# Layer 0's FFN by seven block products, with the context chunk computed ahead of them

## The chip, the cores and the metric

The kernel runs on one core of one Trainium2 chip. The time is device microseconds of one execution, from the runs of the kernel; lower is better. The profile is of one further execution.

## What is computed

Two layers of a trunk over 1024 latent tokens and 256 context tokens, width 1024. Each layer has a mixer (attention) and a SwiGLU FFN of hidden width 2816; after layer 1 only the latent tokens are wanted, so only layer 0's FFN handles the context. Cut to what matters here:

```
def swiglu(h, w_in, w_out):
    g, u = jnp.split(h @ w_in, 2, axis=-1)
    return (jax.nn.silu(g) * u) @ w_out

    x = x + g1 * rms_norm(y, norm_g[l, 1])
    h = rms_norm(x, norm_g[l, 2]) * (1.0 + sc2) + sh2
    x = x + g2 * rms_norm(swiglu(h, ffn_w_in[l], ffn_w_out[l]), norm_g[l, 3])
    if need_ctx:                       # layer 0 only
        xc = xc + cg1 * rms_norm(yc, norm_g[l, 1])
        hc = rms_norm(xc, norm_g[l, 2]) * (1.0 + csc2) + csh2
        xc = xc + cg2 * rms_norm(swiglu(hc, ffn_w_in[l], ffn_w_out[l]), norm_g[l, 3])
```

All inputs are float32. The kernel reaches the accuracy by splitting each matmul operand into a high part in fp32r and the rest, and computing high x high, high x low and low x high: three matmuls for each block (`mm3`).

## The kernel before

The tokens lie in three chunks along the free dimension: `a` and `b` (512 latent tokens each) and `c` (the 256 context tokens). Activations are feature-major: 128 features on the partitions, tokens along the columns. Weights come from HBM as tiles of 128 x 1024 (512 KB), are split by a cast on ScalarE (ACT) into the high part and a subtraction on VectorE (DVE) into the low part (`wsplit`), and are the stationary operands.

There are four pools of buffers: `T` (44 tiles of 128 x 1024), `U` (13 of 128 x 512), `S` (small columns) and `b` (the 8 PSUM banks). The profile calls every tile by its pool: `T`, `U`, `S`, `b`; `scr` is scratch in DRAM. All DMAs are issued from SyncE (SP).

The program is recorded first (`Recorder`) and then issued in an order that a planner finds: it runs a list scheduler with its own costs for the instructions, takes on each engine the earliest recorded of those that are ready, and gives out the buffers of a pool in the order in which they were first used in the recording. The order found is fixed for each engine. Work that runs beside the matmuls (residuals, norms) is written as generators; `tick(us)` advances them at points of the recording and so sets where in the recorded order their work stands. `until(f)` only repeats ticks while recording.

**FFN of layer 0** (`OutFFN.run`). After the output projection of the mixer (`p1`: chunks c and a, `p2`: chunk b), `after` makes the residual and the norm of each chunk, high and low parts in `h2`. Then the 22 hidden tiles `j` run: for each chunk `gu` (gate and up, 48 matmuls over 8 features tiles, Silu, product, split) and `down` of the tile before (24 matmuls, whose results DVE adds to `yacc` from PSUM). One load and one split of the three weight tiles serves all three chunks. The last two tiles run chunk by chunk, c first, so that `finish` (residual, then the norm of layer 1) of c and a runs beside the last matmuls.

**FFN of layer 1** (`WinoFFN.run`), chunks a and b only, by the seven block products of the Winograd form of Strassen's scheme. `after` makes seven sets of four operand tiles, each split into high and low: blocks `B11`, `B21` from chunk a, and `B22`, `T1` to `T4` from a and b; these 28 `T` tiles stay to the end of the tiles. For the first `EARLY` (8) tiles the two products that need only chunk a (`early`) are made while b's sets are not there yet, and parked in `EA` in DRAM. `raw` loads the tiles of gate and up, `prep` makes weight sums on GpSimd (POOL) and splits them, `tile` runs the products of one hidden tile (84 matmuls of 512 columns; 60 for a tile whose first two were made early) and stores the activations to `ACT` in DRAM. Then `down_all` runs the seven products of the down projection, `P1, P5, P6, P3, P7, P2, P4`, 11 steps (`HALF`) of 12 matmuls each: `dload` brings halves of activations (256 KB) and weights four steps ahead, `dprep` makes differences of activations on DVE and weight sums on POOL and splits both, two steps ahead. P5 needs the difference of the two halves of an activation tile, P6, P7 and P4 one more each. `finish` of b starts after P7, that of a after P4.

**Between them**, `odd_mixer` of layer 1: the hook in `f0.run` makes its first loads; then `Proj` runs the projections `(i, chunk)` in a fixed order that starts with weights 9 to 12 (`lead`), chunks c and a, then b.

Of the kernel before, what the change touches and what calls it, by code (L numbers as in the profile page):

```python
# [12 lines left out]
F32 = mybir.dt.float32  # L13
F32R = mybir.dt.float32r
I32 = mybir.dt.int32
AF = mybir.ActivationFunctionType
# [3 lines left out]
P = 128  # L20
D = 1024
KT = D // P
# [3 lines left out]
HID = 2816  # L26
NJ = HID // P
# [16 lines left out]
CHUNKS = {"a": (0, 512), "b": (512, 512), "c": (1024, 256)}  # L44
# [1289 lines left out]
def odd_mixer(pr, h, OT, pre_out):  # L1334


    nc, d = pr.nc, pr.d
# [41 lines left out]
    def evac(i, c, ps):  # L1379
# [17 lines left out]
    ws = [d["od_qk"][i] for i in range(13)]  # L1397
    qorder = lambda i: "ab" if i in (0, 1, 2, 3, 5, 6, 7, 8) else "cab"
    lead = (9, 10, 11, 12)
    order = [(i, c) for i in lead for c in "ca"] + [(i, "b") for i in lead] + \  # L1400
        [(i, c) for i in (4, 0, 1, 2, 3, 5, 6, 7, 8) for c in qorder(i)]
    pj = pr.proj(ws, order, h, evac)
    pj.near = N1
# [139 lines left out]
class OutFFN:  # L1543
# [78 lines left out]
    def begin(self):  # L1622
        for k in "gu":
            self.fetch(k, 0)
        for k in "gu":
            self.cv(k, 0)
        for k in "ogu":
            self.fetch(k, k != "o")
# [85 lines left out]
class WinoFFN(OutFFN):  # L1714
# [4 lines left out]

    EARLY = 8
    HALF = NJ // 2

    def __init__(self, *args):
        super().__init__(*args)
        self.hf, self.sets, self.ready = {}, {}, set()
        self.ACT = self.pr.dram([HID, 1024], F32)
        self.EA = self.pr.dram([self.EARLY * P, 1024], F32)


    def put_set(self, name, k, x):
# [7 lines left out]
            self.ready.add(name)  # L1740

    def after(self, c):
        pr, l, nc = self.pr, self.l, self.pr.nc
        n = CHUNKS[c][1]
        y = self.y.pop(c)
        acc2 = pr.accs()
        yield from pr.g_residual(y, self.acc.pop(c), self.xsrc(c), pr.vec(pr.der[l], 1, c), acc2)
        dst = self.view(self.X1, c)
        for i, t in enumerate(y.tiles):
            pr.load(dst[2 * i * P:2 * i * P + 2 * P, :].rearrange("(k p) n -> p k n", p=P),  # L1750
                    t.rearrange("p (k n) -> p k n", n=n))
        cols = pr.rstd(acc2, n, D)
        yield -RSW
        rb = pr.bcast(cols)
        A, Bv = pr.vec(pr.der[l], 2, c), pr.mvec(l, 3, c)

        def norm(kt):
            pr.stt(y[kt], y[kt], A(kt), rb[:, :n])
            nc.scalar.activation(y[kt], y[kt], AF.Identity, bias=Bv(kt))

        self.hf[c] = y
        if c == "a":
            for kt in range(KT):
                norm(kt)
                self.put_set("B11" if kt < 4 else "B21", kt % 4, y[kt])
                if kt % 2:
                    yield 3.0
            return
        a = self.hf["a"]
        for k in range(4):  # L1770
            norm(k)
            norm(k + 4)
            self.put_set("B22", k, y[k + 4])
            pr.sub(a[k], y[k], a[k])
            yield 2.6
            self.put_set("T1", k, a[k])
            pr.tt(y[k], y[k + 4], y[k], ALU.subtract, eng=nc.gpsimd)
            pr.sub(a[k], y[k + 4], a[k])
            self.put_set("T2", k, a[k])
            yield 2.4  # L1780
            pr.tt(a[k + 4], a[k + 4], a[k], ALU.subtract, eng=nc.gpsimd)
            self.put_set("T3", k, y[k])
            self.put_set("T4", k, a[k + 4])
            yield 2.4
        self.hf.clear()
# [12 lines left out]
        pr.tick(2.7)  # L1798

    def begin(self):  # L1800
        for j in range(2):
            self.fetch("g", j)
        self.gsplit(0)

    def gsplit(self, j):
        hi, lo = self.pr.wsplit(self.raws.pop(("g", j)))
# [52 lines left out]
    def tile(self, j):  # L1859
# [40 lines left out]
        def last():  # L1900
            self.prod(x, "T4", u, 0, False)
            if late:
                pr.add(s5, s1, x)
                pr.mul(act[:, 0:512], sa, s5)
            else:
                pr.mul(act[:, 0:512], sa, x)
            pr.later(lambda: pr.load(self.ACT[j * P:(j + 1) * P, :], act))
            self.last = lambda: None
        self.last = last
# [7 lines left out]
    def dload(self, k):  # L1917
# [16 lines left out]
            pr.load(raw, pr.d["ffn_out"][self.l, j * P:(j + 1) * P, r * 512:(r + 1) * 512])  # L1934
            self.wr.setdefault(k, []).append(raw)

        for a in {"P1": [(0, 0)], "P5": [(0, 1)], "P6": [(1, 1)], "P2": [(1, 0)]}.get(p, []):
            act(*a)
        for b in {"P1": [(0, 0)], "P5": [(1, 0), (1, 1)], "P6": [(0, 0)], "P3": [(0, 1)], "P7": [(0, 0), (1, 0)],
                  "P2": [(0, 1)], "P4": [(1, 1)]}[p]:  # L1940
            w(*b)

    def dprep(self, k):
# [14 lines left out]
            x = k1[:, lo]  # L1958
        elif p == "P5":
            x = k1[:, lo]  # L1960
            pr.sub(x, k1[:, hi], x)
            pr.tt(s, raw[0], raw[1], ALU.add, eng=gp)
        elif p == "P6":
            x = k1[:, lo]
# [19 lines left out]
            self.at.pop(t)  # L1984
            self.at.pop(t + H)

    def down_all(self):
        pr, nc, H = self.pr, self.pr.nc, self.HALF
        self.at, self.wr, self.sw, self.dop = {}, {}, {}, {}
        ya, yb = FMs(pr), FMs(pr)  # L1990
# [7 lines left out]
        for k in range(7 * H):  # L1998
# [8 lines left out]
            for f in range(4):  # L2007
# [2 lines left out]
                pr.mm(ps, wh, xs[:, 0:512], new, False)  # L2010
                pr.mm(ps, wh, xs[:, 512:1024], False, False)
                pr.mm(ps, wl, xs[:, 0:512], False, t == H - 1)
            pr.tick(2.7)
            if t < H - 1:
                continue
            if p == "P7":
# [22 lines left out]
                    pr.sq_add(self.acc["a"], ya[f + 4], 512, 2 * f + 1)  # L2039
            if p == "P7":  # L2040
                pr.long(self.finish("b"))
        pr.long(self.finish("a"))

    def run(self, hook=None):
# [1 line left out]
        pr.drain_slow()  # L2046
        self.p1.run((len(first) * KT - 2, self.p2.start))
        self.p2.run((KT - 3, self.begin))
        pr.until(lambda: "B11" in self.ready)
        for j in range(self.EARLY):  # L2050
            self.early(j)
        self.raw(0)
# [6 lines left out]
        while pr.bg:  # L2059
            pr.tick(0)  # L2060
        self.sets.clear()
        self.down_all()


class FMs:
# [16 lines left out]
def program(ctx, nc, tc, d, out):  # L2082
# [22 lines left out]
        t0, n = CHUNKS[c]  # L2105
        pr.store_fm(out[:, t0:t0 + n], x)

    f0 = OutFFN(pr, 0, "cab", OT0, lambda c: src0[c], put2, norm1)
    f1 = WinoFFN(pr, 1, "ab", OT1, lambda c: X2[:, CHUNKS[c][0]:CHUNKS[c][0] + CHUNKS[c][1]], put3, None)
    m0 = even_mixer(pr, h0, OT0, f0.g_pre)  # L2110
    m1 = odd_mixer(pr, h1, OT1, f1.g_pre)
# [107 lines left out]
```

## Time and profile before

| | us |
|---|---|
| median of 3 runs | 3303.39 (3302.07 to 3306.06) |
| the profiled execution | 3301.75 |
| its span (first to last instruction) | 3300.0 |
| PE busy | 3147.5 (95%) |
| DVE busy | 2156.7 (65%) |
| ACT busy | 1525.0 (46%) |
| POOL busy | 841.1 (25%) |

PE is TensorE's matmuls, PEld its weight loads, which overlap them. Times in the rows are microseconds from the start of the span. Every operation of this kernel goes through one recording helper, so all have one source line (L260), and groups are told apart by their tiles. A few per cent of the matmul records are missing, so counts of matmuls in a window are a little low.

### The profile page before, as it was taken

How to read it: one execution, taken by the hardware profiler on the slowest of the kernel's cores; microseconds unless marked ns; L12 is line 12 of the kernel's file. 1: busy time of each engine (PE TensorE's matmuls, PEld its weight loads, DVE VectorE, ACT ScalarE, POOL GpSimd, SP SyncE). 2: the span in 40 equal slices, each digit the busy share in tenths (PEclk: the TensorE clock that was granted, in tenths of full speed). 3: DMA queues.
4: the chain of work that ended last, by engine and by line, in shares of the span. 5: the costliest groups of instructions: out<-in, count | busy, mean ns of one | idle time of the engine just before them, and what ended most of it. 6: DMA issues, size and time to landing. Idle time of an engine off the chain costs nothing.

```text
span 3300.0 us, 45509 instructions
## 1 busy us (share of the span) xinstructions
PE 3147.5 (95%) x16520; PEld 2605.2 (79%) x16520; DVE 2156.7 (65%) x4083; ACT 1525.0 (46%) x3426; POOL 841.1 (25%) x1091
## 2 busy tenths in 40 slices
PE   7999999999999999999998999899999879999997
PEld 5877777887888888888887887667777768888876
DVE  5569888865544444444469765988995675345984
ACT  4359877864411111111124324777896543334352
POOL 2311100015200000000035643773001554322622
PEclk8999999999999999999999999999999989999998
DMA  6263754354111111111114343533134343224732
GB/s 243 68 220 107 218 167 131 109 186 159 64 39 39 39 39 39 39 39 39 39 59 158 106 140 106 144 109 111 53 115 141 141 153 128 77 83 160 254 109 93
DMA packets 153376, 368.29 MB, mean 112 GB/s; under 512 B 14080, under 2 KB 35264, under 8 KB 153152
## 3 DMA queue, kind: packets, MB, share of 16 engines
q1 hardware_dynamic: 153152, 365.39, 33.6%
q8 instruction: 130, 2.13, 0.3%
q14 instruction: 94, 0.77, 0.1%
HBM read 277.97 MB, written 87.36 MB: 111 GB/s over the span
## 4 chain that ended last, share of the span: by engine, by line
PE 75%; DVE 11%; ACT 4%; POOL 3%; issue 3%; DMA 3%; SPq 0%; POOLq 0%; ACTq 0%; DVEq 0%
PE b L260 75%; DVE T L260 6%; DVE U L260 3%; DVE S L260 3%; ACT T L260 2%; ACT U L260 2%; POOL U L260 2%; POOL S L260 1%; DMA T<-in_ada_w_dram 1%; DMA scr<-T 1%; DMA U<-scr 0%; DMA U<-in_ffn_out_dram 0%; DMA T<-scr 0%; POOL T L260 0%; DMA T<-in_ctxT_dram 0%
## 5 line engine op out<-in xcount | busy, mean ns | idle before, releaser
L260 PE MATMUL b<-T,T 128*128 128x512 f32 (+5 forms) x10618 | 2321.4, 370 | 55.2 <-DVE T L260 22.1
L260 PEld LDWEIGHTS b<-T,T 128*128 128x128 f32 (+2 forms) x10618 | 1837.5, 190 | 404.8 <-ACT T L260 41.3
L260 PE MATMUL b<-U,T 128*128 128x512 f32 (+2 forms) x2752 | 692.3, 376 | 7.3 <-DVE U L260 3.2
L260 DVE TENSOR_TENSOR T<-T,T 128x1024 fp32r<-128x1024 f32 (+4 forms) x475 | 499.7, 1078 | 218.8 <-PE b L260 111.3
L260 PEld LDWEIGHTS b<-U,T 128*128 128x128 f32 x2752 | 465.2, 191 | 78.9 <-issue 5.0
L260 POOL TENSOR_TENSOR U<-U,U 128x512 f32<-128x512 f32 (+1 forms) x141 | 195.5, 1389 | 1114.4 <-PE b L260 806.0
L260 ACT CAST T<-T 128x1024 fp32r<-128x1024 f32 (+3 forms) x362 | 300.7, 845 | 359.4 <-PE b L260 245.4
L260 DVE TENSOR_REDUCE S<-b 128x1 f32<-128x512 f32 (+1 forms) x672 | 374.0, 568 | 63.4 <-PE b L260 58.5
L260 DVE TENSOR_TENSOR U<-U,b 128x512 f32<-128x512 f32 (+3 forms) x228 | 143.5, 630 | 415.9 <-PE b L260 405.9
L260 ACT ACTIVATE T<-b,S 128x512 f32<-128x512 f32 (+1 forms) x640 | 385.5, 609 | 47.9 <-DVE S L260 42.8
L260 DVE TENSOR_TENSOR U<-b,U 128x512 fp32r<-128x512 f32 (+3 forms) x528 | 335.4, 646 | 21.0 <-ACT U L260 16.8
L260 PE MATMUL b<-ident,T 128*128 128x128 f32 x1968 | 316.3, 276 | 23.8 <-ACT T L260 13.2
L260 ACT CAST U<-b 128x512 fp32r<-128x512 f32 (+3 forms) x528 | 291.1, 565 | 87.7 <-PE b L260 84.2
L260 PEld LDWEIGHTS b<-ident,T 128*128 128x128 f32 x1968 | 237.8, 141 | 89.1 <-ACT T L260 31.7
L260 DVE TENSOR_TENSOR T<-T,b 128x512 f32<-128x512 f32 (+1 forms) x524 | 283.1, 594 | 17.1 <-PE b L260 17.1
L260 ACT ACTIVATE U<-b 128x512 f32<-128x512 f32 (+1 forms) x104 | 55.0, 531 | 393.5 <-PE b L260 391.5
L260 POOL TENSOR_TENSOR T<-T,T 128x512 f32<-128x512 f32 x146 | 203.3, 1403 | 118.5 <-DVE T L260 104.9
L260 ACT COPY U<-b 128x512 f32<-128x512 f32 (+3 forms) x175 | 96.2, 550 | 171.9 <-PE b L260 170.2
L260 POOL TENSOR_TENSOR T<-U,T 128x512 fp32r<-128x512 f32 (+2 forms) x51 | 66.4, 1302 | 404.6 <-ACT T L260 371.2
L260 ACT CAST T<-U 128x512 fp32r<-128x512 f32 (+3 forms) x166 | 96.4, 585 | 151.7 <-DVE U L260 110.3
L260 ACT ACTIVATE U<-T 128x512 f32<-128x512 f32 (+1 forms) x174 | 96.1, 577 | 90.7 <-DVE T L260 84.5
L260 ACT ACTIVATION_READ_ACCUMULATOR T<-b,S 128x1 f32 x640 | 132.8, 207 | 0.0
(81 smaller groups left out, 1663.8 us busy)
## 6 DMA issues: line engine op xcount, KB each, us to landing
scr<-T SPq DMA_DIRECT2D x144, 512.0 KB
T<-in_ada_w_dram SPq DMA_DIRECT2D x96, 512.0 KB
T<-in_ffn_in_dram SPq DMA_DIRECT2D x96, 512.0 KB
T<-scr SPq DMA_DIRECT2D x90, 512.0 KB
T<-scr SPq DMA_DIRECT2D x132, 256.0 KB
U<-in_ffn_out_dram SPq DMA_DIRECT2D x99, 256.0 KB
T<-in_w_out_dram SPq DMA_DIRECT2D x32, 512.0 KB
T<-in_ffn_out_dram SPq DMA_DIRECT2D x22, 512.0 KB
```

The lines of the kernel that those rows point to most:

```text
L260: f(*args, **kw)
```

## The change

1. Layer 0's FFN becomes a `WinoFFN` too, for a and b. Its context chunk is computed ahead of the products by a new method `context`: for each of the 22 hidden tiles gate, up and the down of the tile before, at 256 columns, the down results accumulated in four PSUM banks over all tiles and then parked in DRAM (`YC`). The weights of gate, up and down are so loaded and split once for the context and again for the products. In layer 0 no tile is early; `context` takes that place. `finish_c` loads the parked sums back after P2.
2. In both layers the difference that P5 needs is made in `tile` for the first 11 tiles and stored to DRAM (`T1`); P5 loads it in place of the second half of the activations, which is now loaded at P7.
3. Layer 1 makes 12 early tiles instead of 8.
4. `down_all` takes the hook and calls it at the start of P4; the ticks of P2 and P4 are 1.8 instead of 2.7; layer 1's first projections run chunks c and b, then a.

```diff
-    order = [(i, c) for i in lead for c in "ca"] + [(i, "b") for i in lead] + \
+    order = [(i, c) for i in lead for c in "cb"] + [(i, "a") for i in lead] + \
...
-    EARLY = 8
     HALF = NJ // 2
...
         self.ACT = self.pr.dram([HID, 1024], F32)
-        self.EA = self.pr.dram([self.EARLY * P, 1024], F32)
+        self.T1 = self.pr.dram([HID // 2, 512], F32)
+        if "c" in self.chunks:
+            self.EARLY = 0
+            self.YC = self.pr.dram([2 * P, 1024], F32)
+        else:
+            self.EARLY = 12
+            self.EA = self.pr.dram([self.EARLY * P, 1024], F32)
...
+    def context(self):
+        pr, nc = self.pr, self.pr.nc
+        n = CHUNKS["c"][1]
+        act, out = {}, None
+        pr.until(lambda: "c" in self.h2)
+        hi, lo = self.h2["c"]
+        for j in range(NJ + 1):
+            if j < NJ:
+                self.cv("o", j)
+                ps = pr.b()
+                for i, kind in enumerate("gu"):
+                    wh, wl = self.conv.pop((kind, j))
+                    pr.mm3(ps[:, i * n:i * n + n], [(wh[:, k * P:(k + 1) * P], wl[:, k * P:(k + 1) * P], hi[k], lo[k])
+                                                    for k in range(KT)])
+                    pr.tick(n / 100)
+                    if j + 1 < NJ:
+                        if not i:
+                            self.fetch("o", j + 1)
+                        self.cv(kind, j + 1)
+                        self.fetch(kind, j + 2)
+                sg, a = pr.U()[:, :n], pr.U(F32R)
+                nc.scalar.activation(sg, ps[:, 0:n], AF.Silu)
+                pr.mul(sg, sg, ps[:, n:2 * n])
+                act[j] = (a[:, 0:n], a[:, n:2 * n])
+                pr.split(sg, *act[j])
+            if j == 0:
+                continue
+            if out is None:
+                out = [pr.b() for _ in range(4)]
+            ah, al = act.pop(j - 1)
+            wh, wl = self.conv.pop(("o", j - 1))
+            for f in range(KT):
+                ps = out[f // 2][:, (f % 2) * n:(f % 2) * n + n]
+                s = slice(f * P, (f + 1) * P)
+                pr.mm(ps, wh[:, s], ah, j == 1 and f % 2 == 0, False)
+                pr.mm(ps, wh[:, s], al, False, False)
+                pr.mm(ps, wl[:, s], ah, False, j == NJ)
+            pr.tick(n / 100)
+        self.h2.pop("c")
+        for i in range(2):
+            y = pr.T()
+            for k in range(2):
+                nc.scalar.copy(y[:, k * 512:(k + 1) * 512], out[2 * i + k])
+            pr.load(self.YC[i * P:(i + 1) * P, :], y)
+
+    def finish_c(self):
+        pr = self.pr
+        n = CHUNKS["c"][1]
+        y = self.yacc["c"] = FM(pr, n, F32)
+        for i, t in enumerate(y.tiles):
+            pr.load(t, self.YC[i * P:(i + 1) * P, :])
+        yield -3.0
+        acc = self.acc["c"] = pr.accs()
+        for kt in range(KT):
+            pr.sq_add(acc, y[kt], n, kt)
+        yield -3.5
+        yield from self.finish("c")
...
+            if j < self.HALF:
+                d = pr.U()
+                pr.sub(d, act[:, 512:1024], act[:, 0:512])
+                pr.later(lambda: pr.load(self.T1[j * P:(j + 1) * P, :], d))
             pr.later(lambda: pr.load(self.ACT[j * P:(j + 1) * P, :], act))
...
-        for a in {"P1": [(0, 0)], "P5": [(0, 1)], "P6": [(1, 1)], "P2": [(1, 0)]}.get(p, []):
+        for a in {"P1": [(0, 0)], "P6": [(1, 1)], "P7": [(0, 1)], "P2": [(1, 0)]}.get(p, []):
             act(*a)
+        if p == "P5":
+            pr.load(self.at[t][:, 0:512], self.T1[t * P:(t + 1) * P, :])
...
             x = k1[:, lo]
-            pr.sub(x, k1[:, hi], x)
             pr.tt(s, raw[0], raw[1], ALU.add, eng=gp)
...
-            pr.tick(2.7)
+            pr.tick(2.7 if p != "P2" and p != "P4" else 1.8)
+            if k == 6 * H and hook:
+                hook()
...
+            if p == "P2" and "c" in self.chunks:
+                pr.long(self.finish_c())
...
-        pr.until(lambda: "B11" in self.ready)
+        if "c" in self.chunks:
+            self.context()
+        else:
+            pr.until(lambda: "B11" in self.ready)
         for j in range(self.EARLY):
             self.early(j)
...
-    f0 = OutFFN(pr, 0, "cab", OT0, lambda c: src0[c], put2, norm1)
+    f0 = WinoFFN(pr, 0, "cab", OT0, lambda c: src0[c], put2, norm1)
```

## Rows read from the trace of the kernel before

**Rows 1.** The page: busy shares, and the 40 slices of PE and its clock.
```profile
PE 3147.5 (95%) x16520; PEld 2605.2 (79%) x16520; DVE 2156.7 (65%) x4083; ACT 1525.0 (46%) x3426; POOL 841.1 (25%) x1091
...
PE   7999999999999999999998999899999879999997
```

**Rows 2.** The page's chain of work that ended last, share by engine.
```profile
PE 75%; DVE 11%; ACT 4%; POOL 3%; issue 3%; DMA 3%; SPq 0%; POOLq 0%; ACTq 0%; DVEq 0%
```

**Rows 3.** Windows: length; PE, PEld, DVE, ACT, POOL busy; PE clock; DMA share; GB/s.
```profile
870.00:1660.00 790.00, 790.00 (x4138) 682.46 (x4138) 366.35 (x623) 132.72 (x194) 0.00 (x0) 1.00 0.12 39
```

**Rows 4.** Timeline, layer 0's FFN: start, length of the group, engine, operation, count.
```profile
1643.58 5.60 PE L260 MATMUL b<-U,T 128*128 128x512 f32 x24
...
1649.02 5.92 PE L260 MATMUL b<-T,T 128*128 128x256 f32 x48
...
1649.93 2.54 DVE L260 TENSOR_TENSOR T<-T,T 128x1024 fp32r<-128x1024 f32 x2
...
1654.78 3.04 PE L260 MATMUL b<-U,T 128*128 128x256 f32 x24
```

**Rows 5.** Timeline of ACT, layer 0's FFN: the context's Silu of two neighbouring tiles.
```profile
991.30 0.39 ACT L260 ACTIVATE U<-b 128x256 f32<-128x256 f32 x1 [2.05 <-PE b L260]
...
1032.60 0.39 ACT L260 ACTIVATE U<-b 128x256 f32<-128x256 f32 x1 [2.05 <-PE b L260]
```

**Rows 6.** Windows, end of layer 0's FFN and layer 1's projections.
```profile
1680.00:1830.00 150.00, 137.56 (x642) 112.01 (x641) 125.66 (x202) 60.52 (x103) 68.12 (x99) 0.94 0.33 114
...
1830.00:1950.00 120.00, 117.38 (x582) 98.44 (x581) 91.36 (x155) 37.76 (x60) 81.44 (x164) 1.00 0.36 121
```

**Rows 7.** Timeline of DVE, layer 0's residuals and layer 1's norms.
```profile
1705.12 0.47 DVE L260 SCALAR_TENSOR_TENSOR U<-T,der,b 128x256 f32<-128x256 f32 x1
...
1783.97 1.41 DVE L260 SCALAR_TENSOR_TENSOR T<-T,der,b 128x512 f32<-128x512 f32 x2 [1.52 <-PE b L260]
...
1785.29 1.29 DVE L260 TENSOR_TENSOR T<-T,T 128x512 f32<-128x512 f32 x2
```

**Rows 8.** Layer 1, early tiles: windows, then the timeline of PE.
```profile
2592.00:2655.00 63.00, 59.12 (x265) 48.66 (x264) 43.02 (x60) 37.22 (x61) 29.73 (x38) 0.97 0.38 141
...
2655.00:2692.00 37.00, 21.28 (x78) 15.89 (x77) 29.89 (x34) 17.92 (x28) 24.96 (x16) 0.77 0.32 108
...
2583.25 1.87 PE L260 MATMUL b<-ones,U 128*128 128x1 f32 x8 [3.47 <-POOL U L260]
...
2654.81 4.92 PE L260 MATMUL b<-T,T 128*128 128x512 f32 x21
...
2667.88 2.08 PE L260 MATMUL b<-T,T 128*128 128x512 f32 x4 [8.15 <-ACT T L260]
...
2677.15 7.18 PE L260 MATMUL b<-T,T 128*128 128x512 f32 x22 [7.20 <-DVE T L260]
```

**Rows 9.** Layer 1, full tiles: the window, and POOL's sums in it by form.
```profile
2810.00:3030.00 220.00, 220.00 (x973) 182.15 (x972) 90.15 (x104) 78.03 (x105) 62.42 (x45) 1.00 0.28 91
...
L260 POOL TENSOR_TENSOR T<-T,T 128x512 f32<-128x512 f32 x34 | 47.5, 1410 | 79.6 <-DVE T L260 78.8
```

**Rows 10.** Layer 1, down products: windows; DVE by form at 3045:3155 (three), 3210:3275 (one).
```profile
3040.00:3160.00 120.00, 113.25 (x494) 92.07 (x493) 118.67 (x119) 46.62 (x83) 73.31 (x44) 1.00 0.70 237
...
3160.00:3275.00 115.00, 115.00 (x519) 95.44 (x518) 70.20 (x109) 53.41 (x96) 17.59 (x22) 1.00 0.31 101
...
3050.00:3060.00 10.00, 8.96 (x40) 7.06 (x39) 10.00 (x11) 6.75 (x12) 5.50 (x4) 1.00 1.05 386
...
L260 DVE TENSOR_TENSOR T<-T,T 128x512 fp32r<-128x512 f32 x53 | 57.5, 1123 | 0.0
...
L260 DVE TENSOR_TENSOR T<-T,T 128x512 f32<-128x512 f32 x33 | 40.5, 1268 | 0.1
...
L260 DVE TENSOR_TENSOR T<-T 128x512 f32<-128x512 f32 x8 | 8.6, 1090 | 0.0
...
L260 DVE TENSOR_TENSOR T<-U,T 128x512 fp32r<-128x512 f32 x15 | 10.2, 681 | 0.7 <-ACT T L260 0.7
```

More of the change, by code (lines that the diff above doesn't have):

```diff
@@ L1742, in after @@
     def after(self, c):
+        if c == "c":
+            yield from super().after(c)
+            return
         pr, l, nc = self.pr, self.l, self.pr.nc
@@ L1800, in begin @@
     def begin(self):
+        if "c" in self.chunks:
+            super().begin()
+            return
         for j in range(2):
@@ L1985, in dprep, with down_all @@
             self.at.pop(t + H)
-    def down_all(self):
+    def down_all(self, hook):
         pr, nc, H = self.pr, self.pr.nc, self.HALF
@@ L2048, in run @@
         self.p2.run((KT - 3, self.begin))
-        pr.until(lambda: "B11" in self.ready)
+        if "c" in self.chunks:
+            self.context()
+        else:
+            pr.until(lambda: "B11" in self.ready)
         for j in range(self.EARLY):
@@ L2061, in run @@
         self.sets.clear()
-        self.down_all()
+        self.down_all(hook)
 class FMs:
```

## The prediction

> **What bounds the kernel now.** I read the engines' busy shares and the slices first: TensorE (PE) is busy for 95% of the span and is the digit 9 in nearly every slice, at full granted clock [rows 1]. Then the chain that ended last: three quarters of it is PE work, 11% VectorE (DVE) [rows 2]. So the kernel is a stream of matmuls with a few holes, and a change is worth the matmuls it removes, less the holes it opens. Where matmuls go, the windows say: from 870 to 1660 us (layer 0's FFN) PE is busy for 790 of 790 us, DVE for 366, POOL for none [rows 3]. The holes nearest to the change are 12.4 us at 1680 to 1830 and 2.6 us at 1830 to 1950 (layer 0's end and layer 1's projections, [rows 6]), 15.7 us at 2655 to 2692 with the clock at 0.77 on average [rows 8], and 6.75 us at 3040 to 3160, where DVE is busy for 118.7 of 120 us [rows 10].
>
> The price of a matmul comes from the timeline: 24 of 512 columns start at 1643.58 and the next group at 1649.02, so 5.44/24 = 0.2267 us each; 48 of 256 columns take 1649.02 to 1654.78, 0.120 us each [rows 4]. By these a hidden tile of layer 0 costs 72 x (0.120 + 2 x 0.2267) = 41.3 us, and two Silu instructions of neighbouring tiles are 1032.60 - 991.30 = 41.3 us apart [rows 5]: the stage runs at this pace and nothing else.
>
> **The change part by part.**
>
> *Layer 0's matmuls, on the path.* Before, a hidden tile has 72 matmuls of 512 columns for chunk a and as many for b: 144. After, seven products of 12 matmuls for gate and up (84), and 7 x 11 down steps of 12, over 22 tiles 42 each: 126. The context's 72 of 256 columns stay. So 18 x 22 = 396 matmuls go: 396 x 0.2267 = **-89.8 us**. The Trainium skill, TensorE: Matmul & The Clock Gate (section Wait — 56ns, not 53.3ns?), gives 215.7 ns start to start at 512 columns on the warm clock; these groups show 226.7. By the page the term would be an estimated -85.4 us; the row decides.
>
> *The context alone.* 22 steps of 72 x 0.120 = 8.64 us, 190 us in all, the same matmuls as before. What is new is that each step must bring and split three weight tiles in 8.64 us instead of 41.3. DMA: 1.57 MB, 182 GB/s; a window of the down products moved 386 [rows 10]. DVE: three splits of 1.27 us [rows 4] and two 256-column ops of some 0.4, 4.6 us. ACT: less. Each alone is hidden. But under the same stretch lie the norms of a and b and the 28 operand sets, which before existed in layer 1 only. There b's chain ran from the sum of its squares at 2583 until PE had its sets at 2677, 94 us, with DVE busy for 43 of the 63 us from 2592 and 29.9 of the next 37 [rows 8]: some 73 us, less the early tiles' own 14, about 60. In eleven steps (95 us) that is 60 + 11 x 4.6 = 111 us of DVE against 95 of PE: about 16 short, less what the two tiles prepared ahead cover. The sets also hold 28 of the 44 large buffers and the context's operands 4, which leaves 12 for weights, and near the end of the sets 8. Both ends: 3 us (the whole queue of 190 us has 190 - 101 = 89 us of DVE free, so only bursts show) and 35 us (16 short, and as much again as layer 1's hole for operands that come late, with its slow clock). I take **+14**, nearer to the 16. The wait that this adds is PE's, in order, so every later context matmul stands behind it; DVE's splits stand behind set operations that wait for POOL.
>
> *From context to tiles.* Tile 0's first product needs one load and a split; its third two POOL sums and a split more. The weight buffers come free only as the context's last two steps end, and SP has the two stores of the parked context sums among the loads. From 0 (all of it done while the context's last steps run) to 8 (a load at 182 GB/s, 2.9, two POOL sums of 1.4 [rows 9], two splits of 1.27): **+4**. Behind a late load stand tile 1's loads on SP, 19 us before they are needed.
>
> *The tiles.* The 14 full tiles of layer 1 ran with PE busy for 220 of 220 us, DVE at 90, POOL at 62 [rows 9]; layer 0's 22 are the same code. The early difference adds one DVE op of some 1 us and 256 KB to 11 of 22 tiles: hidden under 19 us of matmuls (under 13.6 in layer 1's early tiles). **0**; without that cover 11 us per layer.
>
> *First sum made early, in layer 1.* At 3040 to 3160 DVE is the bound: P5's differences take 1.09 us, 33 others 1.27 (P6's 11, and those of P7 and P4, which the planned order does ahead of their turn), 53 splits 1.12 [rows 10]. P5 loses 11 differences, 12 us of DVE, nearly twice the hole of 6.75 us. The load of the other half moves to P7, where DVE had room (PE busy for 115 of 115 us at 3160 to 3275, DVE for 70 [rows 10]); P5 still loads three pieces a step, its first half now into a buffer that P1 has read eleven steps earlier. What can bring the hole back is the planned order, which may pull other differences into the room. From -6.75 to 0: **-5**. In layer 0 the same products run with the difference already made: 0 to 6.75, **+2**.
>
> *Layer 0's last two products and the handover.* Here b's and c's residuals and next norms now run under P2 and P4. DVE there: 22 steps of two splits, 44 x 0.60 = 26 us (0.68 recorded [rows 10], starts some 0.08 closer); additions from PSUM 8 x 0.60 = 5; b's finish 24 multiply-adds at 0.66 and 8 additions at 0.64 [rows 7], 21, up to 26 where an addition takes 1.27 beside POOL; c's, 32 ops of half that width at about 0.47 [rows 7], 15; the lambda sums 2. Together 69 to 74 us against 22 x 2.72 = 60 of PE, so DVE ends 9 to 14 late. Before, a's norm (16 such ops, 11 us) also came after the FFN's last matmul, and the holes were 15 us [rows 6]; b's first projections, 4 x 24 x 0.2267 = 22 us, can run while c is unfinished, a's turn now being last as b's was. From -2 (c no longer competes with the additions of each down tile) to 30 (15 late and the old holes once more): **+8**. The new order of layer 1's first projections and the smaller ticks under P2 and P4 only set in which order this work is queued, and are in this term.
>
> *Twelve early tiles in layer 1.* PE stood from 2659.7 to 2667.9 and 2670.0 to 2677.2 and then ran 22 matmuls in 7.18 us instead of 5 [rows 8]: 15.3 us plus about 2. Four more early tiles move 4 x 24 x 0.2267 = 21.8 us of matmuls into that hole. They cost DVE, and the sets behind it, 4 x 1.9 = 7.6 us (a split, an addition). Sets at 2677 + 7.6 = 2685, PE's early work over at 2660 + 22 = 2682: the tiles begin 8 us later with 21.8 us less to do. -18 (hole and clock wholly gone) to -6: **-14**.
>
> Sum: -89.8 + 14 + 4 + 2 + 8 - 14 - 5 = -80.8. The profiled execution took 3301.75 us (span 3300.0); 3301.75 - 80.8 = 3221. The median of the runs is 1.6 higher, so **3222.6 us**; the rivals' times are on the median too.
>
> **The rivals.** *Everything stays covered.* All lower ends: -89.8 + 3 + 0 + 0 - 2 - 18 - 6.75 = -113.6, 3190 us. For it: PE never waited in 870 to 1660, DVE half idle. Against: layer 1's same chain did leave a hole.
>
> *DVE becomes the bound in both crowded places.* Context +35, handover +30, +8, +6.75: -89.8 + 79.75 - 14 - 5 = -29, 3274 us. For it: a split that takes 0.68 us takes 1.12 where POOL works beside it [rows 10], and layer 0's FFN had no POOL work at all before [rows 3]. Against: the context can work DVE's arrears off over 190 us. The Trainium skill, GPSIMD Engine Reference (section Key points), says the same of it: POOL shares its SBUF interfaces with VectorE, and contention falls on VectorE ops with two SBUF inputs; the trace agrees, 1.12 against 0.68.
>
> *The early tiles and the early sum give nothing*, since DVE, not the wait, sets when the sets are there: -80.8 + 19 = -61.8, 3241.6 us. For it: DVE is dense up to 2677; against, the hole is as long as the added matmuls.
>
> *Slower: the context is bound by its weights.* One mechanism, in the 190 us alone: with 12 buffers, and 8 for a while, a step's loads cannot start until matmuls free buffers, and load, split and matmul run one after the other. The rest of the sum is -94.8, so it decides from 94.8/22 = 4.3 us a step: 12.9 us, 122 GB/s. The 108 GB/s of layer 1's hole [rows 8] would make a step 14.6 us, 22 x 5.9 = 130 us more: 3339 us. For it: the hole of layer 1 with the same 28 sets held. Against: 6 buffers hold the step's own splits, so 6 are left for what comes next, and 386 GB/s were seen.
>
> **How the numbers follow.** Forecast 0.60, all covered 0.12, DVE twice 0.14, nothing from layer 1's edits 0.07, weights 0.07. The forecast's own terms spread to about 3198 to 3250. For 8 in 10 I leave out the last few microseconds of the lowest case (0.06) and above half of the DVE case and all of the weights' (0.14): 3192 to 3272. Less than 0.2% (6.6 us) can't be told from no change here. Faster by more: 0.60 + 0.12 + 0.07 + 0.13 = 0.92; within: 0.01 from each of the last two = 0.02; slower 0.06.
>
> **What would show it.** The context should appear as some 200 us of 256-column matmuls with PE at 9 or more after its first 100 us; tiles of 19 us with PE full; P5 without DVE at 10; the largest hole of layer 0 at P4 and the first projections; none above 5 us before layer 1's tile 0. I am wrong if a context step takes over 10 us throughout, if PE waits in the 22 tiles, or if the hole at layer 1's early tiles is as long as before.

## The result, and the profile after

The changed kernel takes 3260.53 us (median of 4 runs, 3256.51 to 3265.07) against 3304.03 of before on the same chip: ratio 0.9869, 95% interval 0.9852 to 0.9886. Faster by 43.5 us; 80.8 were forecast. The time lies in the range, 38 us above the forecast. The profiled execution, the fastest of the four, took 3256.51 us, its span is 3254.7.

The page after: busy shares, the slices of PE and of its clock, and the chain by engine; then the clock's slices of before, which [rows 1] leaves out.

```profile
PE 3067.7 (94%) x16124; PEld 2538.1 (78%) x16124; DVE 2216.2 (68%) x3927; ACT 1712.9 (53%) x3710; POOL 1059.4 (33%) x1235
...
PE   7998999999799999999987999899999899999997
...
PEclk8999999999999999999998999999999999999998
...
PE 54%; DVE 10%; POOL 3%; ACT 2%; issue 2%; DMA 0%; POOLq 0%; SPq 0%; ACTq 0%; DVEq 0%
```

```profile
PEclk8999999999999999999999999999999989999998
```

The 396 matmuls are gone (16520 to 16124). PE's share fell all the same, from 95% to 94% [rows 1]: PE is busy for 79.8 us less and stands for 34.5 us more (187.0 against 152.5), so there are more holes. That the busy time did not fall by the 89.8 us of the matmuls goes with the clock: its mean is 0.979 after 0.982, by which, as an estimate, 0.021 x 3254.7 - 0.018 x 3300.0 = 9 us more are lost. The 54% of the chain is no such sign: this chain was followed back only to 916 us and its shares add up to 71%, of which PE has three quarters, as before [rows 2]. The windows of the stages (columns as in [rows 3]) say where.

```profile
830.00:945.00 115.00, 93.53 (x717) 90.63 (x716) 86.10 (x104) 59.84 (x90) 36.16 (x41) 0.93 0.41 132
945.00:1056.00 111.00, 105.32 (x855) 102.88 (x855) 51.52 (x61) 44.90 (x60) 2.27 (x2) 1.00 0.51 169
1060.00:1475.00 415.00, 415.00 (x1836) 343.72 (x1835) 184.52 (x220) 154.70 (x215) 118.97 (x85) 1.00 0.32 108
1475.00:1585.00 110.00, 106.70 (x457) 87.41 (x456) 99.84 (x98) 40.98 (x75) 70.65 (x44) 0.97 0.70 248
1585.00:1664.00 79.00, 79.00 (x351) 65.40 (x350) 53.05 (x75) 43.36 (x78) 11.05 (x7) 1.00 0.37 120
1664.00:1800.00 136.00, 108.43 (x505) 89.09 (x504) 108.94 (x173) 59.98 (x108) 70.83 (x113) 0.89 0.35 121
2620.00:2645.00 25.00, 18.61 (x76) 14.56 (x74) 25.00 (x33) 16.38 (x29) 9.06 (x6) 0.86 0.40 138
2655.00:2692.00 37.00, 36.64 (x162) 30.03 (x161) 22.30 (x24) 12.05 (x16) 24.13 (x15) 1.00 0.56 188
3000.00:3120.00 120.00, 116.60 (x501) 95.56 (x500) 107.04 (x109) 47.76 (x87) 70.22 (x44) 0.97 0.72 252
```

The first two are the context, and 21.5 + 5.7 us of holes; the third the tiles, without a hole. The fourth and the last hold P1, P5, P6 and the start of P3 in layer 0 and layer 1, each with one wait of 3.3 us at the end of P6. Between them, 1664 to 1800 holds P4 and layer 1's first projections, with 27.6 us of holes, where the answering stretch of before lost 12.4 [rows 6]. In layer 1 the hole of [rows 8] at 2655 to 2692 is gone and 6.4 us are left at 2620 to 2645.

**A context step.** The timeline of one, all engines; in brackets the idle time before and what ended it.

```profile
986.16 0.38 ACT L260 ACTIVATE U<-b 128x256 f32<-128x256 f32 x1 [0.87 <-PE b L260]
...
986.60 2.89 PE L260 MATMUL b<-T,T 128*128 128x256 f32 x22 [0.47 <-ACT U L260]
989.33 3.04 PE L260 MATMUL b<-U,T 128*128 128x256 f32 x24
...
992.21 3.28 PE L260 MATMUL b<-T,T 128*128 128x256 f32 x26
...
995.52 0.38 ACT L260 ACTIVATE U<-b 128x256 f32<-128x256 f32 x1 [0.87 <-PE b L260]
```

Two Silu are 9.36 us apart, not 72 x 0.120 = 8.64. The group of 26 is gate's 24 matmuls and up's first two; then PE stands until the Silu of gate has ended, and does up's other 22. Gate and up are the halves of one PSUM bank in `context`; before, each had a bank. If it costs as much in every step, that is 22 x 0.72 = 15.8 us.

**The first third of the context** has one long wait; the timelines of PE and of DVE ahead of it:

```profile
886.05 0.40 PE L260 MATMUL b<-T,T 128*128 128x256 f32 x2
895.91 7.37 PE L260 MATMUL b<-T,T 128*128 128x256 f32 x39 [9.47 <-DVE T L260]
```

```profile
881.24 6.47 DVE L260 TENSOR_TENSOR T<-T,T 128x512 fp32r<-128x512 f32 x7
...
888.30 10.50 DVE L260 TENSOR_TENSOR T<-T,T 128x512 fp32r<-128x512 f32 x12
```

The rows merge neighbouring forms. Taken singly, fourteen splits, sums and differences of 512 columns, for the operand sets that b's norm releases, stand ahead of the split of up's weights (1024 columns, from 893.58 to 895.86 us), for which PE waits.

**The handover**, PE's timeline. `ones` matmuls sum columns for a norm, `ident` ones spread its result.

```profile
1654.68 10.82 PE L260 MATMUL b<-T,T 128*128 128x512 f32 x47
1665.34 0.95 PE L260 MATMUL b<-ones,U 128*128 128x1 f32 x8
...
1688.79 1.87 PE L260 MATMUL b<-ones,U 128*128 128x1 f32 x8 [7.19 <-POOL U L260]
...
1710.93 3.69 PE L260 MATMUL b<-T,T 128*128 128x512 f32 x15 [2.26 <-DVE T L260]
1716.96 0.43 PE L260 MATMUL b<-ident,S 128*128 128x128 f32 x2 [2.33 <-POOL S L260]
...
1763.36 1.87 PE L260 MATMUL b<-ones,U 128*128 128x1 f32 x8 [3.81 <-POOL U L260]
1768.43 4.42 PE L260 MATMUL b<-T,T 128*128 128x256 f32 x22 [3.20 <-DVE T L260]
```

POOL's timeline:

```profile
1637.42 10.13 POOL L260 TENSOR_TENSOR U<-U,U 128x512 f32<-128x512 f32 x6
1667.24 0.20 POOL L260 TENSOR_TENSOR S<-S 128x4 f32<-128x4 f32 x1 [19.69 <-DVE S L260]
```

POOL finished b's squares at 1647.5 (the last six sums from 1637.42, 10.13 us), but b's first `ones` matmul ran at 1665, when P2 was done. P2 holds four PSUM banks and P4's parked group the other four. From there PE, in order, stands at one small matmul after another, for POOL's sums of squares above all.

### The profile page after: what moved, and what is told of

Its sections match the earlier page's. It is cut to its first block, busy times and chain, and to the rows that moved or that the text cites. A ratio compares the mean times of both kernels' runs of the same rounds, so it can differ in the third digit from the quotient of the medians.

```text
span 3254.7 us, 45863 instructions
## 1 busy us (share of the span) xinstructions
PE 3067.7 (94%) x16124; PEld 2538.1 (78%) x16124; DVE 2216.2 (68%) x3927; ACT 1712.9 (53%) x3710; POOL 1059.4 (33%) x1235
## 4 chain that ended last, share of the span: by engine, by line
PE 54%; DVE 10%; POOL 3%; ACT 2%; issue 2%; DMA 0%; POOLq 0%; SPq 0%; ACTq 0%; DVEq 0%
PE b L260 54%; DVE T L260 6%; DVE S L260 2%; DVE U L260 2%; POOL S L260 1%; ACT T L260 1%; ACT U L260 1%; POOL U L260 1%; DMA T<-in_ada_w_dram 0%; POOL T L260 0%; POOLq L2297 0%; ACT L260 0%; DVE neglam L260 0%; SPq L260 0%; POOLq L260 0%
## 5 line engine op out<-in xcount | busy, mean ns | idle before, releaser
L260 PE MATMUL b<-T,T 128*128 128x512 f32 (+5 forms) x11278 | 2477.9, 372 | 70.8 <-DVE T L260 26.9
L260 PEld LDWEIGHTS b<-T,T 128*128 128x128 f32 (+1 forms) x11278 | 1969.9, 191 | 450.9 <-ACT T L260 44.4
L260 DVE TENSOR_TENSOR T<-T,T 128x512 fp32r<-128x512 f32 (+4 forms) x742 | 760.3, 1055 | 301.6 <-ACT T L260 205.0
L260 ACT CAST T<-T 128x512 fp32r<-128x512 f32 (+2 forms) x588 | 462.7, 807 | 460.5 <-DVE T L260 187.3
L260 PE MATMUL b<-U,T 128*128 128x512 f32 (+3 forms) x1696 | 443.1, 366 | 8.4 <-ACT U L260 4.4
L260 POOL TENSOR_TENSOR T<-T,T 128x512 f32<-128x512 f32 x220 | 307.1, 1407 | 266.3 <-DVE T L260 246.1
L260 DVE TENSOR_TENSOR U<-b,U 128x512 fp32r<-128x512 f32 (+3 forms) x528 | 336.0, 648 | 19.4 <-ACT U L260 15.4
L260 PEld LDWEIGHTS b<-U,T 128*128 128x128 f32 x1696 | 266.7, 192 | 37.6 <-ACT U L260 7.8
L260 ACT COPY U<-b 128x512 f32<-128x512 f32 (+4 forms) x233 | 130.4, 560 | 248.2 <-PE b L260 240.1
L260 ACT CAST T<-U 128x512 fp32r<-128x512 f32 (+2 forms) x210 | 123.2, 592 | 179.8 <-DVE U L260 114.9
L260 POOL TENSOR_TENSOR T<-T 128x512 f32<-128x512 f32 x44 | 61.8, 1405 | 367.5 <-PE b L260 223.6
L260 DVE TENSOR_TENSOR T<-U,T 128x512 fp32r<-128x512 f32 (+3 forms) x170 | 115.7, 690 | 55.6 <-ACT T L260 55.2
```

Of the source, the lines that this page charges most:

```text
L260: f(*args, **kw)
```

## The experiments

All kernels are the changed one with the edit shown. The table gives the lengths of the stages in the profiled executions, between marks that every kernel has: layer 0's first ffn_in load, the context's last 256-column matmul, layer 0's last Silu, layer 1's first V matmul (320 columns), layer 1's first ffn_in load, its last Silu, the last matmul.

```
kernel                  context  tiles 0  down 0, handover  attention  early, tiles 1  down 1   time, ratio to before
after                     285.1    414.5             442.2      594.2           496.1   234.2   3260.5  0.9869 [0.9852, 0.9886]
e1_two_banks              269.7    414.5             442.8      594.4           498.7   233.1   3244.8  0.9817 [0.9802, 0.9831]
e6_small_ticks            274.3    414.5             443.1      592.8           497.5   234.2   3247.6  0.9822 [0.9806, 0.9838]
e2_p4_first               286.1    414.5             436.4      593.6           497.6   233.0   3251.4  0.9837 [0.9823, 0.9852]
e11_two_sums_alone        290.8    414.5             435.5      593.3           498.6   233.0   3256.8  0.9844 [0.9828, 0.9861]
e9_swap_two_sums          289.0    414.5             421.7      593.4           498.5   233.9   3241.1  0.9809 [0.9794, 0.9824]
e4_sums_on_dve            286.3    414.5             436.6      594.0           497.4   227.3   3247.6  0.9824 [0.9809, 0.9839]
e3_first_sum_late         286.7    415.9             443.4      590.6           498.3   234.5   3258.3  0.9858 [0.9841, 0.9874]
e5_held_differences       285.0    414.5             453.0      593.1           498.5   234.9   3271.1  0.9889 [0.9875, 0.9904]
e7_early_eight            288.1    414.5             443.2      593.2           509.1   232.9   3274.4  0.9910 [0.9895, 0.9925]
e8_combined               254.3    414.5             425.2      593.1           498.8   227.8   3206.2  0.9704 [0.9690, 0.9719]
e10_combined_two_sums     257.5    414.5             413.6      594.1           496.3   226.5   3195.6  0.9662 [0.9648, 0.9676]
e12_combined_early14      254.3    414.5             415.1      593.1           498.3   227.4   3194.7  0.9659 [0.9645, 0.9673]
```

Kernels that leave a stage alone show its scatter: 285 to 291 us in the context, 442 to 443 in the handover, 591 to 594 in the attention, 496 to 499 in layer 1's tiles, 233 to 234 in its down products. The times come from several chips, on which the kernel before took 3303.4 to 3307.1 us, so a few microseconds between two times say little; the stages say more.

**The bank of gate and up.**

```diff
-                ps = pr.b()
+                gu = [pr.b()[:, :n], pr.b()[:, :n]]
...
-                nc.scalar.activation(sg, ps[:, 0:n], AF.Silu)
-                pr.mul(sg, sg, ps[:, n:2 * n])
+                nc.scalar.activation(sg, gu[0], AF.Silu)
+                pr.mul(sg, sg, gu[1])
```

> Gate and up of a context step get a PSUM bank each instead of the two halves of one. Theory A (the third matmul of up waits for the Silu that reads the other half of its bank): the Silu distance in the steady context falls from 9.36 to 8.64 us, the waits on ACT U in 945 to 1056 us vanish, 22 x 0.72 = 15.8 us less: 3260.5 - 15.8 = 3245 us. Rival B (the step is set by its weights or by VectorE, the Silu is only the last to come): the wait moves to another buffer, the distance stays at 9.2 or more, the time within 4 us of 3260.5.

The context is 15.4 us shorter, the time 3244.84 us. PE in the steady part of the context, window:

```profile
945.00:1040.00 95.00, 95.00 (x794) 95.00 (x793) 47.58 (x55) 41.54 (x55) 0.81 (x1) 1.00 0.57 185
```

Theory A. In the trace the third matmul of up waits for a semaphore that the Silu's engine raises. The planner takes only overlapping columns for a dependency, so it had put the Silu behind up's second matmul without a price. The Trainium skill, PSUM — Partial Sum Buffer (section PSUM bank collisions raise a hardware error), wants two engines kept apart by semaphores by bank and group of 32 partitions, not by address. The trace agrees: 0.72 us a step, for other columns of the same bank. A PSUM tile of this kernel is one whole bank, so no run here tells a wait by bank from a wait by tile.

**Smaller portions of background work in the context.**

```diff
-                    pr.tick(n / 100)
+                    pr.tick(1.4)
...
-            pr.tick(n / 100)
+            pr.tick(1.4)
```

> In the context stage the background work (norms and operand sets of a and b) is queued in portions of 1.4 us instead of 2.56 after each group of matmuls, so the context's own weight splits come sooner in VectorE's order. Theory A (the first third of the context, 830 to 945 us, loses its 11 us of waits and its lower clock because splits of the next weights stand behind operand sets): PE waits there fall to 4 us or less, 8 to 12 us gained: 3250 us. Rival B (the total of VectorE's work before the tiles is what counts): the sets come late and PE stands before tile 0 or later in the context, nothing gained or up to 10 us lost: 3260 to 3270 us. The wait for the Silu of each step is not touched, so its 15.8 us stay by both.

10.8 us shorter, as A had it. PE's waits from 830 to 945 us (total, count, longest), first after, then this kernel:

```profile
PE b L260 <- ACT U L260: 9.8, 10, 3.9
PE b L260 <- DVE T L260: 9.5, 1, 9.5
PE b L260 <- POOL S L260: 1.7, 1, 1.7
PE b L260 <- DVE U L260: 0.5, 1, 0.5
```

```profile
PE b L260 <- ACT U L260: 6.9, 10, 1.8
PE b L260 <- POOL S L260: 3.1, 2, 2.6
```

The long wait is gone, and nothing is late at tile 0 (tiles 414.5 as before). From 830 to 945 us DVE is busy for 87.5 us, against 86.1 in the kernel after: the order of its work was at fault, not its amount.

**P4 before P2, and shorter sums of squares.** With P4 first, the second half of the activations is loaded at P4, a's sums start there, and four banks are free meanwhile.

```diff
-    PRODS = ("P1", "P5", "P6", "P3", "P7", "P2", "P4")
+    PRODS = ("P1", "P5", "P6", "P3", "P7", "P4", "P2")
...
```

> The order of the last two down products is exchanged: P4 before P2, in both layers. While P4 runs, the four banks of P4's group are in use and four are free; in the kernel after, P2 and the parked group held all eight, so that b's first small matmuls (column sums for the norm) stood until P2's end at about 1664 us. Theory A (banks): b's chain starts some 30 us sooner, is finished under P4 and P2, and PE's waits from 1664 to 1800 us (27.4 us and a slower clock) shrink by 15 to 20 us: 3243 us. Rival B (VectorE is the bound there, with 109 of 136 us busy): the waits move into P4 and P2, the time within 5 us of 3260.5. Layer 1's tail has the same chain of b: within 2 us either way by both.

b's first `ones` matmul came 172 us after layer 0's last Silu instead of 190, but the stage is only 5.8 us shorter, a third of what A wanted and near B's 5 (the time, 3251.4, lies between the two): with the banks free PE stood for the same chains a little later. The next two split the sums:

```diff
-                self.acc["b"] = pr.accs(1 if self.next_norm else 2)
+                self.acc["b"] = pr.accs(2)
...
-        acc2 = pr.accs() if self.next_norm else None
+        acc2 = pr.accs(2) if self.next_norm else None
...
```

> P4 before P2, and the sums of squares of the FFN's output split in two halves, one on GpSimd and one on VectorE, instead of seven in a row on GpSimd (10 to 11.5 us for each of b and a, twice). Theory A (after the exchange it is the length of each chunk's chain, GpSimd's sums above all, that lets PE stand at the small matmuls): each chain 5 us shorter, PE's waits from 1640 to 1800 us fall from 22 us to 14 or less, 3243 us, 8 less than with the exchange alone. Rival B (VectorE is the bound, busy for 112 of 135 us there, and gets 16 more operations): no gain on the exchange alone, 3251 us or more.

> P2 before P4 as in the kernel after; only the sums of squares of the FFN's output (before and after the residual) are split between GpSimd and VectorE. Theory A (the two edits of the handover are two causes: while P2 holds the last banks b's small matmuls cannot start, however soon its sums are there): 6 us or less gained, 3255 us, against the 20 of both edits together. Rival B (the long row of seven sums on GpSimd was all of it and the exchange of P2 and P4 is worth nothing beside it): some 20 us gained, 3241 us.

Alone the split gave 6.7 us in its stage, near A's 6 and far from B's 20 (3.7 in the time, as the context of this run was 5.7 longer); with the exchange it gave 20.5, more than 5.8 + 6.7. A holds in both runs: banks and the length of the chains are two causes, and either hides part of the other. Windows of 158 us around the handover: after, exchange, split, both.

```profile
1642.00:1800.00 158.00, 130.43 (x602) 107.31 (x601) 121.21 (x187) 67.89 (x122) 76.15 (x117) 0.90 0.37 129
```

```profile
1644.00:1802.00 158.00, 137.92 (x643) 114.13 (x642) 129.50 (x196) 71.17 (x126) 85.98 (x119) 0.91 0.41 142
```

```profile
1648.00:1806.00 158.00, 142.02 (x677) 118.73 (x677) 123.21 (x206) 70.46 (x126) 54.56 (x99) 0.91 0.40 139
```

```profile
1647.00:1805.00 158.00, 149.25 (x736) 125.12 (x735) 127.01 (x213) 74.44 (x134) 64.10 (x125) 0.96 0.43 149
```

DVE is busier with both (127.0 against 121.2) while PE's holes fall from 27.6 to 8.8 us: DVE was not the bound here.

**The weights' sums of the down products on DVE.**

```diff
-        gp = pr.nc.gpsimd
+        gp = pr.nc.vector
```

> The sums and differences of the weights for the down products P5, P6, P3 and P7 (44 in each layer) go from GpSimd to VectorE. Theory A (VectorE is late at P6 and P3 because its operations with two SBUF inputs take 1.0 to 1.3 us beside GpSimd and 0.68 without): the operations fall to about 0.7 us, P6 needs 22 x 0.68 + 11 x 0.66 + 11 x 0.66 = 29.5 us of VectorE in 30, the holes at the end of P6 (3.3 us in layer 0, 3.3 us and a slower clock in layer 1, some 10 in all) go: 3252 us. Rival B (it is the number of VectorE's operations): 44 more a layer, 30 us each, make VectorE late in P6 and P7 too: 3270 us or more.

Both layers' holes go, 5.6 and 6.8 us in their stages, more than A's 10 in all. Windows of the kernel, then DVE by form, after and here, over 67 us that hold P6 in layer 1 (count, busy, mean ns):

```profile
1478.00:1588.00 110.00, 110.00 (x487) 91.09 (x486) 96.34 (x157) 49.93 (x87) 0.00 (x0) 1.00 0.72 250
3000.00:3120.00 120.00, 120.00 (x531) 99.34 (x530) 101.50 (x164) 56.26 (x99) 0.00 (x0) 1.00 0.71 252
```

```profile
L260 DVE TENSOR_TENSOR T<-T,T 128x512 f32<-128x512 f32 x33 | 41.2, 1290 | 0.2
L260 DVE TENSOR_TENSOR T<-T,T 128x512 fp32r<-128x512 f32 x29 | 28.5, 1022 | 0.0
```

```profile
L260 DVE TENSOR_TENSOR T<-T,T 128x512 fp32r<-128x512 f32 x41 | 27.0, 689 | 5.4 <-ACT T L260 5.1
L260 DVE TENSOR_TENSOR T<-T,T 128x512 f32<-128x512 f32 x33 | 21.6, 686 | 0.0
L260 DVE TENSOR_TENSOR U<-U,U 128x512 f32<-128x512 f32 x11 | 7.5, 686 | 0.0
```

With 55 instructions more in the 120 us, DVE is busy for 5.5 us less.

**The first sum late again**, as before the change.

```diff
-        if p == "P5":
-            pr.load(self.at[t][:, 0:512], self.T1[t * P:(t + 1) * P, :])
...
             x = k1[:, lo]
+            pr.sub(x, k1[:, hi], x)
...
```

> Undoes one part: the difference of activations that P5 needs is made in P5 again, in both layers; no difference is stored in the tiles. Theory A (what makes VectorE late at the end of P6 is the length of its operations beside GpSimd, and the 11 freed operations were only replaced by others that the planned order does ahead of their turn): the down products of each layer take within 2 us of the kernel after, 3260 us. Rival B (the step did take 11 us a product off VectorE, as forecast, and the holes of 3.3 and 6.5 us are what is left of longer ones): 5 to 7 us more in each layer, 3271 us.

The down stages are 1.2 and 0.3 us longer, about their scatter, and the time is 3258.3: A. The early sum is worth 1 us a layer or less. Yet it does shorten the waits: here they are 7.1 us in layer 0 and 5.7 in layer 1, against 3.3. Layer 1's window of this run, the one wait of the kernel after, and the 5 us behind that wait:

```profile
3000.00:3120.00 120.00, 114.31 (x494) 93.23 (x493) 118.59 (x119) 46.06 (x82) 73.68 (x44) 0.99 0.70 239
```

```profile
3100.38 14.96 PE L260 MATMUL b<-T,T 128*128 128x512 f32 x52 [3.26 <-DVE T L260]
```

```profile
3101.00:3106.00 5.00, 5.00 (x13) 3.93 (x12) 4.97 (x5) 0.00 (x0) 3.77 (x4) 0.50 0.25 86
```

Behind the one long wait the granted clock is at 0.50, the lower of its two levels (1.2 GHz), and PE does 13 matmuls in 5 us instead of 22. In this run, with several shorter waits, it is 0.99 over the window. In the kernel before, the 6.75 us of [rows 10] were shorter waits too, the longest this one, and the clock was 1.00:

```profile
3145.81 3.06 PE L260 MATMUL b<-T,T 128*128 128x512 f32 x12 [2.15 <-DVE T L260]
```

What the early sum takes off the waits, the clock takes back.

**Differences held to their turn**, to see whether the others that the planned order does early fill the room:

```diff
             pr.sub(x, k2[:, lo], x)
+            pr.nc.ops[-1][5].update(self.mark[-1:])
...
```

> The kernel after, but the planned order may issue a difference of activations for P6, P7 or P4 only once the first matmul of the third step before it is issued; nothing else is changed. Theory A (with the sums on VectorE the holes went, so it is the slower operations beside GpSimd): the holes of 3.3 and 6.5 us at the end of P6 stay, since P5 and P6 need 22 splits each at 1.02 and 11 differences at 1.29 us, some 59 of 60 us, 3256 to 3261 us. Rival B (the differences of P7 and P4 that the planned order does ahead of their turn in P6 make VectorE late): the holes go, 5 us in each layer, 3250 us.

Neither. The holes at P6 do shrink (3.3 to 2.5 us and to 2.4), which speaks for B, but layer 1's stage is no shorter for it (234.9; PE stands for 3.7 us under P4 instead, for POOL's part of b's norm), and the handover is 10.8 us longer. PE's waits there (1642 to 1800), after and held:

```profile
PE b L260 <- POOL U L260: 12.2, 3, 7.2
PE b L260 <- POOL S L260: 7.0, 4, 2.6
```

```profile
PE b L260 <- POOL U L260: 12.4, 4, 7.0
PE b L260 <- POOL S L260: 12.1, 4, 5.2
```

The likely cause, which no run tests by itself: the eleven differences of P4, done early at the price of P6, had lightened P4. From 1664 to 1730 us DVE now makes 16 sums and differences of that form against 8. Each theory had overlooked the other end of the move.

**Eight early tiles.**

```diff
-            self.EARLY = 12
+            self.EARLY = 8
```

> Undoes one part: eight tiles of layer 1 begun ahead instead of twelve. Theory A (the four more tiles move 21.8 us of matmuls into the hole before tile 0): from layer 1's first ffn_in load to its down products 11 to 15 us longer, 3273 us. Rival B (VectorE's operand sets alone set when the tiles can start, and the gain of 12.8 us came from elsewhere in this stage): within 4 us of 3260.5.

13.0 us longer in its stage: A.

**Together.**

> All four edits tried before together: a bank each for gate and up in the context, P4 before P2, the weights' sums of the down products on VectorE, background portions of 1.4 us in the context. If the four holes are separate, as their stages say (-15.4 and -10.8 us in the context, -6.5 and -6.9 in the down products, -5.9 and -1.6 after them): 3260.5 - 47 = 3213 us. Rival (in the context the two gains are one: with the Silu's wait gone VectorE's arrears are hit sooner): the context gains 20 instead of 26, 3220 us.

> The four edits combined before (3206.2 us) and the sums of squares split between GpSimd and VectorE. If the 13 us that the split gave on top of the exchange are the waits of 20.7 us at 1620 to 1900 us, which the four edits left: 3193 us. If VectorE, which does the down products' weight sums too here, has no room for the split sums under P4 and P2: 3203 us or more.

> As the combination with split sums, with 14 tiles of layer 1 begun ahead instead of 12. The hole that is left at the early tiles is 6.4 us with a clock of 0.80 for some 25 us after it. If it is a matter of matmuls at hand (two tiles more are 10.9 us): 5 us less than the same with 12. If VectorE's sets (3.8 us more of other work ahead of them) are the bound there now, or the hole lies before the early tiles' last ones: within 3 us of it.

The four edits gave 3206.2 us, 7 below the 3213 of their sum by stages: 30.8 in the context, 17.0 and 6.4 in the down stages. The context gained more than the 26.2 of its two edits alone, where the rival had less; why is not shown. With the split sums 3195.6, near the 3193 expected, 3.4% less than before and beside the change's own 1.3%. Fourteen early tiles add nothing measurable (3194.7): the matmuls moved, the end of the stage did not. DVE's sets are not the bound: their last split starts at 2586.9 us with twelve early tiles and at 2587.1 with fourteen, and the last early tile has its Silu at 2604.1 and 2614.7. The hole that is left lies among the early tiles, from 2573 to 2581 us with twelve, with 6.4 and 6.1 us of waits for ACT; matmuls that come behind it cannot fill it. The page of the kernel with split sums:

```profile
PE 3052.8 (96%) x16160; PEld 2533.6 (79%) x16160; DVE 2184.2 (68%) x4030; ACT 1718.1 (54%) x3710; POOL 918.5 (29%) x1127
```

## Why the prediction was right in sign and 38 us short

In the profiled executions the saving is 3301.75 - 3256.51 = 45.2 us. Layer 1's first V matmul stands 32.3 us earlier than before, where the terms of layer 0 gave 61.8; the 29.5 us between them are most of the error.

- **Layer 0's matmuls, -89.8.** Right: the 22 tiles run at PE's pace without a hole, 407.0 us from first to last Silu in all kernels but the one that makes no early sum.
- **The context, +14: mis-sized, 31.** The step that failed was "the same matmuls as before" at 8.64 us. It priced the matmuls and not where they write: one bank for both halves costs 15.4 us, which no rival had. The arrears of DVE, on which the +14 rested, cost 10.8 by the order of the queue. With both edits the stage gives back 30.8, the 31 that is taken here for what it cost.
- **Context to tiles, +4, and the tiles, 0.** Neither cost anything: the third window has no hole.
- **The first sum, -5 in layer 1: -0.4.** The stage took 234.6 us before and takes 234.2. The step that failed is "P5 loses 11 differences, 12 us of DVE, nearly twice the hole": the waits went from 6.75 us to 3.3 and not to 0, and the clock behind the one long wait took back what was gained, which this term did not have. The step took the length of the operations as given. The same operations take 0.69 us where POOL is idle and 1.02 to 1.29 beside it; freed room was filled by other differences at that price, as the prediction had itself named for what could bring the hole back. It used 1.12 against 0.68 for a rival only. In layer 0, +2 was 5.6, the hole of 3.3 and a slower clock after it, which the sums on DVE give back.
- **The handover, +8: mis-sized.** What is left of the 32.3 is -32.3 + 89.8 - 31 - 5.6 = 21 us, a remainder and not a measurement. The step that failed is the sum of DVE's work, 69 to 74 us against 60 of PE. PE stands for the chains, sums of squares on POOL and banks that P2 holds, and both edits together give back 20.5 us with DVE busier than before.
- **Twelve early tiles, -14.** Right in size: undone, 13.0. Its working had the sets ready 3 us after PE's early work (2685 against 2682); measured, their last split starts at 2642.1, 17 us before the Silu of the last early tile (2659.1), so tile 0 does not stand for them, and 6.4 us of holes stayed among the early tiles.

The time lies between the forecast and the rival with DVE as the bound in both places (3274 us), nearer to it. Its sizes (35 and 30) are nearer to 31 and 21 than the forecast's 14 and 8; its mechanism, DVE as the bound, explains 10.8 of them at most, so that nearness is in part luck. Of the signs named, the tiles, and the last hole before tile 0 (3.9 us, under 5), came as said. The context took some 231 us, not 200, DVE is still at 10 in the last two thirds of P5, with the hole at the end of P6, and layer 0's longest wait was the 9.47 us in the context, not at P4. That a step would not take over 10 us held (9.36), and was too loose a test: 0.72 us in each of 22 steps passed it.

Open: why the exchange and the split, and the two edits of the context, give more together than the sum of each alone. That layer 1's attention takes 1.3 us more (594.2 after 592.9) is within its scatter.

## What to carry to other kernels

When code is rewritten around the same matmuls, list for each buffer who reads it while another engine still writes its neighbour: a shared bank is a wait in every step. Price a vector operation by what runs beside it, and move work to the slower engine only if the faster one keeps its speed. In a chain of small dependent steps, add up latencies and banks held, not the busy time of one engine.

## What the hardware showed that was not expected

DVE did more work in less time: 164 instructions in 101.5 us against 109 in 107.0, with POOL busy for 0 instead of 70 us. The Trainium skill, SBUF — State Buffer (section SBUF: two separate sides), calls the pair of ports that the two share an exclusive lock, held for a whole instruction, for vector operations with two SBUF inputs; 1290 ns against 686 is what it cost here. Taken one by one, the trace agrees with the whole instruction: of the 62 operations of these two forms from 3045 to 3112 us in the kernel after, 34 took 0.68 to 0.69 us and 28 took 1.64 to 1.82, none between, and each of the 28 overlaps an operation of POOL.

A hole can cost more than its length: after the wait of 3.3 us in P6 of layer 1 the clock fell (0.97 over the 120 us, against 1.00 without the wait), and removing the wait gave 6.8 us. Before, 6.75 us of waits in the same products, none over 2.15, left it at 1.00 [rows 10].
